# Gated linear attention: the TensorE pieces of two heads interleaved, the scores issued in front of the state updates

## The chip, the cores and the metric

The kernel runs on one core of one Trainium2 chip. The metric is device time in microseconds (us), the median over runs. The engines are named as the profile names them: PE is the matrix engine (TensorE), PEld its weight loads, DVE the vector engine, ACT the scalar engine, POOL the engine GpSimd, and SP the engine that issues the DMAs. PE writes its products to PSUM, which has eight banks of 128 x 512 float32; this kernel gives four of them to a pool "pm" and four to a pool "pd".

## The reference

One encoder layer is computed for two sequences of 512 tokens (a "prompt" and a "sample", called s = 0 and s = 1 in the kernel), model width 1024: a half-step SwiGLU, then a mixer of two head groups, then a second half-step SwiGLU and a gated per-layer embedding, each with a layer norm. The change lies in one of the mixer's head groups, the bidirectional gated linear attention with 4 heads, key width 64, value width 128, in chunks of 64 tokens (8 chunks a sequence). Cut to what matters, one direction of one head is:

```python
scores = einsum('bnihd,bnjhd->bnhij', q * exp(cum - mid), k * exp(mid - cum))
scores = where(mask, scores, 0.0)                       # triangle of each chunk
o_intra = einsum('bnhij,bnjhe->bnihe', scores, v)
upd = einsum('bnjhd,bnjhe->bnhde', k * exp(last - cum), v)
state_{n+1} = chunk_decay_n[..., None] * state_n + upd_n   # over the 8 chunks, in order
o_inter = einsum('bnihd,bnhde->bnihe', q * exp(cum), state_n)
o = o_intra + o_inter
```

The forward and the backward direction are added, normalised per head (RMS), multiplied by a gate, and go with the attention heads' output into one output projection `w_out`.

## The kernel before, in words

**PE's order is written out by hand.** The order of all other engines is set by the scheduler of the tile framework, which also hands out buffers from pools and adds the waits. Python generators each issue one piece of PE work (with the work of other engines that belongs to it) and then yield. A `Ticker` steps the main stream: one tick is three matmuls of a projection. `weave` takes one piece of a side stream, then as many ticks as keep the two in step up to a target tick.

In the stage of the change the main stream is the output projection (`wout`, the matmuls at line L703): the attention heads' half for both sequences, then, from tick 384 on, the linear attention's half for s = 0. The side stream is `order()`: 64 pieces woven into the 81 ticks from 334 to 415, so that after a piece there are one or two ticks, 1.27 on average.

**One sequence of the linear attention** is four generators in `gla(s)`:

- `pre(hp)`, five pieces for a pair of heads: loads, then four times two small matmuls (L986), whose exponentials (ACT, L173) scale queries and keys. The scaled `qk1` of both heads (q1, k1, both directions stacked on the partitions) is written by DVE at L1004.
- `one(h)`, three pieces for a head. First: the loads of the values `gvh` and the gates `Gh` (L1012, L1013, eight DMAs on SP), the transposes of k1 (L1018) and the copy of the result to `kT` (ACT, L1020). Second: the eight state updates U = kT x gvh (L1025, two banks), then the chain of states `W`: two copies on ACT (L1032, L1033), six forward and six backward steps on DVE that depend on one another (L1035, L1037), and two multiplications by the decay on POOL (L1038, L1039). Third: the scores S (L1047, two banks) and their masked copy into `A` (DVE, L1049).
- `two_a(h)`, one piece: the output o, one bank, twelve matmuls (L1058 with A and gvh, L1061 with q1 and the states W); then a square on ACT (L1064), a sum on DVE (L1066), the RMS (DVE L778, ACT L173, DVE L183 to L185), and four DVE instructions that write the gated result to `Gh` (L1069).
- `two_b(h)`, one piece: the transposes of `Gh` (L1076), and their copies into `mixG` (ACT L1077, DVE L1078), which the output projection reads.

The texts below call the pieces of a pair of heads 0 and 1: kT0, U0, S0, kT1, U1, S1 (the three pieces of `one`), o0 and o1 (`two_a`), p (the five of `pre` for the next pair; the first holds loads alone), t0 and t1 (`two_b`). A pair is 15 pieces, the last pair (which has no `pre` behind it) 10, with three empty pieces ahead of its last transposes. Before the change a pair's order was

```python
yield from A[1](0)      # kT0 U0 S0
yield from A[1](1)      # kT1 U1 S1
yield from A[2](0)      # o0
yield from A[2](1)      # o1
yield from A[0](1)      # p p p p p
yield from A[3](0)      # t0
yield from A[3](1)      # t1
```

There are four pairs: two for s = 0 (`A`) and two for s = 1 (`B`). The products of the pieces kT, U, S, o, p and t all take banks of the pool pd, four in number; a piece that asks for a bank waits until the last reader of some earlier product is done.

Of the kernel before, what the change touches and what calls it, by code (L numbers as in the profile page):

```python
# [20 lines left out]
NT = 4  # L21
# [9 lines left out]
PLAN = dict(s0=102,  # L31
            s1=112,
            d0=(8, 14, 20, 26, 32),
            sB=(52, 56, 60, 75, 77),
            d1=(90, 96, 102, 108, 117),
            A=(157, 159, 160),
            seg=((2, 132), (2, 142), (18, 160), (18, 170), (43, 193), (43, 216), (178, 334)),
            b=(4, 3),
            end=415)
# [671 lines left out]
class Middle:  # L711
# [246 lines left out]
    def gla(self, s):  # L958
        nc, L = self.nc, self.L
        f, bw = slice(0, 64), slice(64, 128)  # L960
        T = {}
# [45 lines left out]
        def one(h):  # L1007
            cs = slice(h * 128, (h + 1) * 128)
            gv = self.m2("gvh", shape=(128, NT, 128))
            G = self.m2("Gh", shape=(128, NT, 128))  # L1010
            for t in range(NT):
                nc.sync.dma_start(gv[:, t], self.spill["gv", s][t][:, cs])  # L1012
                nc.sync.dma_start(G[:, t], self.spill["G", s][t][:, cs])  # L1013
            q1, k1 = T["z", h][:, 0], T["z", h][:, 1]
            R = T["R", h]
            b = L.bank_d()
            for t in range(NT):
                nc.tensor.transpose(b[:, t * 128:(t + 1) * 128], k1[:, t * 128:(t + 1) * 128], L.ident)  # L1018
            kT = self.m2("kT", shape=(128, NT, 128))
            nc.scalar.activation(kT.rearrange("p a n -> p (a n)"), b, AF.Copy)  # L1020
            yield
            U = [L.bank_d().rearrange("p (c n) -> p c n", c=4) for _ in range(2)]
            for c in range(8):
                rw = slice(64 * (c % 2), 64 * (c % 2) + 64)
                nc.tensor.matmul(U[c % 2][:, c // 2], kT[rw, c // 2], gv[rw, c // 2], start=True, stop=True)  # L1025
            if h % 2 == 0:
                T["W"] = self.m8("W", (128, 2, 8, 128))
            W = T["W"][:, h % 2]
            nc.gpsimd.memset(W[f, 0], 0.0)
            nc.gpsimd.memset(W[bw, 7], 0.0)  # L1030
            up = lambda c, rd: U[c % 2][rd, c // 2]
            nc.scalar.activation(W[f, 1], up(0, f), AF.Copy)  # L1032
            nc.scalar.activation(W[bw, 6], up(7, bw), AF.Copy)  # L1033
            for c in range(1, 7):
                nc.vector.scalar_tensor_tensor(W[f, c + 1], W[f, c], R[f, c:c + 1], up(c, f), ALU.mult, ALU.add)  # L1035
                cb = 7 - c
                nc.vector.scalar_tensor_tensor(W[bw, cb - 1], W[bw, cb], R[bw, cb:cb + 1], up(cb, bw), ALU.mult, ALU.add)  # L1037
            nc.gpsimd.tensor_tensor(W[f, 1:8], W[f, 1:8], R[f, 1:8].unsqueeze(2).to_broadcast([64, 7, 128]), ALU.mult)  # L1038
            nc.gpsimd.tensor_tensor(W[bw, 0:7], W[bw, 0:7], R[bw, 0:7].unsqueeze(2).to_broadcast([64, 7, 128]), ALU.mult)  # L1039
            yield  # L1040
            A = T["A"][:, h % 2]
            S = [L.bank_d().rearrange("p (a n) -> p a n", a=NT) for _ in range(2)]
            for t in range(NT):
                ts = slice(t * 128, (t + 1) * 128)
                for dr in range(2):
                    rd = slice(64 * dr, 64 * dr + 64)
                    nc.tensor.matmul(S[dr][:, t], k1[rd, ts], q1[rd, ts], start=True, stop=True)  # L1047
            for dr in range(2):
                nc.vector.copy_predicated(A, self.L.mask[:, dr].unsqueeze(1).to_broadcast([128, NT, 128]), S[dr])  # L1049
            T["h", h] = gv, G, W, A  # L1050
            yield

# [84 lines left out]
def build(tc, d, outs):  # L1137
    nc = tc.nc
    ctx = ExitStack()
    with ctx:  # L1140
# [37 lines left out]
        with ExitStack() as mctx:  # L1178
            M = Middle(L, mctx, h1)
            o0, q0, o1, q1 = [], [], [], []  # L1180

            def projections():
                yield from M.akvz(0, o0)
                yield from M.aq(0, q0)
                yield from M.g_gr(0)
                yield from M.g_gr(1)
                yield from M.akvz(1, o1)
                yield from M.aq(1, q1)
                yield from M.g_gv(0)
                yield from M.g_gqk(0)  # L1190
                yield from M.g_gv(1)
                yield from M.g_gqk(1)
                yield from M.wout(0, 1)
                yield from M.wout(1, 1)
                yield from M.wout(0, 0)
            main = Ticker(projections())
            main.to(28)
            main.weave(L.flip(1, 1, "h1T"), 8, 60)

            def rows1():  # L1200
                m = M.m8("h1", (128, 4, 512))
                for c in (slice(0, 512), slice(512, 1024)):
                    for j in range(2):
                        src = d["lnw"][j:j + 1, c]
                        nc.sync.dma_start(m[:, j], src.partition_broadcast(128).rearrange("p a n -> p (a n)"))
                    for n in range(2 * NT):
                        s, t = divmod(n, NT)
                        h = m[:, 2 + n % 2]
                        nc.sync.dma_start(h, z1[s][t][:, c])
                        L.affine(h, m[:, 0], m[:, 1])  # L1210
                        nc.sync.dma_start(h1[s][t][:, c], h)
                        if n % 2:
                            yield
            main.weave(rows1(), 8, 100)
            main.to(PLAN["s0"])
            main.weave(M.qk_stacks(0, q0, o0[0], (None, 0, 1, 2, 3)), 5, PLAN["s1"])
            main.to(130)
            M.preload()
            A, B = M.gla(0), M.gla(1)
            A00 = A[0](0)  # L1220
            attn = M.attn((o0[1], o1[1]), lambda: main.n > 256)
            sB = M.qk_stacks(1, q1, o1[0], (0, 1, 2, None, 3))
            d0, d1 = M.decay(0, o0[2]), M.decay(1, o1[2])
            ins = sorted([(k, d0) for k in PLAN["d0"]] + [(k, sB) for k in PLAN["sB"]] + [(k, d1) for k in PLAN["d1"]]
                         + [(k, A00) for k in PLAN["A"]], key=lambda x: x[0])
            side = merge(attn, ins)
            p = 0
            for k, n in PLAN["seg"]:
                main.weave(side, k - p, n)
                main.to(n)  # L1230
                p = k
            assert next(side, None) is None, p
            def order():
                yield from A00
                for _ in range(PLAN["b"][0]):
                    yield
                yield from A[1](0)
                yield from A[1](1)
                yield from A[2](0)
                yield from A[2](1)  # L1240
                yield from A[0](1)
                yield from A[3](0)
                yield from A[3](1)
                yield from A[1](2)
                yield from A[1](3)
                yield from A[2](2)
                yield from A[2](3)
                yield from B[0](0)
                yield from A[3](2)
                yield from A[3](3)  # L1250
                yield from B[1](0)
                yield from B[1](1)
                yield from B[2](0)
                yield from B[2](1)
                yield from B[0](1)
                yield from B[3](0)
                yield from B[3](1)
                yield from B[1](2)
                yield from B[1](3)
                yield from B[2](2)  # L1260
                yield from B[2](3)
                for _ in range(PLAN["b"][1]):
                    yield
                yield from B[3](2)
                yield from B[3](3)
            main.weave(order(), 60 - len(PLAN["A"]) + PLAN["b"][0] + PLAN["b"][1], PLAN["end"])
            main.end()

            def ln2(s, fast):
                m, r = L.ln_scale(s, LN_EPS, fast)  # L1270
                for t in range(NT):
                    L.ln_z(s, t, m, r)
                    nc.sync.dma_start(z2[s][t], L.Y[s, t])
            ln2(0, True)
            main = Ticker(M.wout(1, 0))
            main.to(14)
            raw = L.rest()
            main.weave(L.flip(0, 2, "h2T", raw), 8, 32)
            main.end()
            ln2(1, False)  # L1280
# [164 lines left out]
```

## Time and profile before

| | us |
|---|---|
| median of 3 runs | 2014.57 (2014.25 to 2017.84) |
| the profiled execution's own time | 2012.7 |
| its span, first to last instruction | 2010.6 |
| PE busy in the span | 1893.7 (94%) |
| DVE busy | 1379.6 (69%) |
| the four pairs of heads, from 1038.19 to 1170.68 | 132.49 |
| PE busy in them | 115.17 |
| DVE busy in them | 108.39 |

The profile is of one execution. Starts and durations in a timeline row are in us from the span's start; a bracket at the end of a row is the idle time of that engine just before the row and what ended it. A group "x4" is four like instructions in a row, and a matmul's end is modelled, so that neighbouring groups overlap a little. In a row of stretches come the stretch, its length, the busy time of PE, PEld, DVE, ACT and POOL with their instruction counts, the TensorE clock granted (1.00 is full speed), and the DMA share and GB/s.

### The profile page before, as it was taken

Reading aid. Unit: us, or ns where it says so; the run is one execution under the profiler, and the core shown is the slowest. Engines: PE = TensorE matmul, PEld = TensorE weight load, DVE = VectorE, ACT = ScalarE, POOL = GpSimd, SP = SyncE. Lnnn points to the kernel's source line nnn. Section 1 sums busy time; section 2 is a strip of 40 time slices with the busy share of each in tenths; the row PEclk is TensorE's granted clock in tenths of the full one; section 3 lists DMA queues with packets and bytes.
Section 4 is the critical chain, followed back from the end, with each engine's and each line's share of the span. In section 5 each row is a group of like instructions: output and inputs, shape, how many; then the busy total and the mean of one; then the engine's idle time right before and its main releaser. Section 6 shows DMA issues by size and latency. Waiting matters only on the chain. (4 is left out here: it accounts for less than half of the span.)

```text
span 2010.6 us, 25530 instructions
## 1 busy us (share of the span) xinstructions
PE 1893.7 (94%) x8838; PEld 1544.4 (77%) x8838; DVE 1379.6 (69%) x2100; ACT 883.1 (44%) x1670; POOL 945.1 (47%) x710
## 2 busy tenths in 40 slices
PE   7999999999899987989998898998999999799899
PEld 5788888888688766877876676877888888588687
DVE  7857566574565875788778888777566574645973
ACT  5445444444221534757744256335444444221342
POOL 0665665555671352342233345554665545841243
PEclk9999999999899998999999998999999999899999
DMA  4425434479664544222442233555434479466232
GB/s 175 152 105 182 167 139 168 163 271 355 250 235 164 178 157 160 84 79 89 142 142 89 90 132 120 179 172 198 164 137 168 158 292 351 184 239 240 74 116 84
DMA packets 119936, 339.02 MB, mean 169 GB/s; under 512 B 12672, under 2 KB 49280, under 8 KB 114432
## 3 DMA queue, kind: packets, MB, share of 16 engines
q1 hardware_dynamic: 119808, 337.39, 46.8%
q8 instruction: 70, 1.15, 0.2%
q14 instruction: 58, 0.48, 0.1%
HBM read 227.24 MB, written 110.10 MB: 168 GB/s over the span
## 5 line engine op out<-in xcount | busy, mean ns | idle before, releaser
L138 POOL TENSOR_TENSOR w<-raw,w 128x512 fp32r<-128x512 f32 (+1 forms) x372 | 507.9, 1376 | 802.6 <-ACT w L137 741.9
L137 ACT ACTIVATE w<-raw 128x512 fp32r<-128x512 f32 (+1 forms) x586 | 362.0, 624 | 426.5 <-PE pm L535 91.3
L424 PE MATMUL pm<-X,w 128*128 128x512 f32 x1848 | 439.0, 395 | 21.3 <-ACT X L137 8.1
L424 PEld LDWEIGHTS pm<-X,w 128*128 128x128 f32 x1848 | 350.1, 190 | 101.8 <-ACT X L137 8.8
L266 POOL TENSOR_TENSOR raw<-raw 128x512 f32<-128x512 f32 x240 | 346.3, 1452 | 165.1 <-DMA raw<-in_wgu 96.4
L424 PE MATMUL pd<-X,w 128*128 128x512 f32 x1320 | 310.7, 394 | 2.9 <-DVE w L138 2.2
L138 DVE TENSOR_TENSOR w<-raw,w 128x512 fp32r<-128x512 f32 x214 | 218.8, 1028 | 113.4 <-ACT w L137 103.6
L424 PEld LDWEIGHTS pd<-X,w 128*128 128x128 f32 x1320 | 249.6, 189 | 58.5 <-DVE w L138 3.0
L535 PE MATMUL pm<-w,XB 128*128 128x512 f32 x864 | 205.6, 399 | 14.2 <-issue 7.5
L535 PEld LDWEIGHTS pm<-w,XB 128*128 128x128 f32 x864 | 166.3, 193 | 51.8 <-issue 7.8
L703 PE MATMUL pm<-w,h1T 128*128 128x512 f32 (+1 forms) x768 | 183.9, 383 | 16.2 <-ACT gr L745 16.2
L138 DVE TENSOR_TENSOR hs<-sg,hs 128x512 fp32r<-128x512 f32 (+1 forms) x182 | 145.2, 818 | 46.6 <-ACT hs L137 45.3
L137 ACT ACTIVATE hs<-sg 128x512 fp32r<-128x512 f32 (+1 forms) x182 | 98.5, 562 | 172.4 <-DVE sg L387 67.9
L703 PEld LDWEIGHTS pm<-w,h1T 128*128 128x128 f32 x768 | 137.0, 196 | 38.2 <-ACT gr L745 16.4
L535 PE MATMUL pd<-w,XB 128*128 128x512 f32 x648 | 151.6, 393 | 6.4 <-DVE Y L522 5.7
L535 PEld LDWEIGHTS pd<-w,XB 128*128 128x128 f32 x648 | 122.6, 190 | 33.4 <-DVE Y L522 6.9
L522 DVE TENSOR_TENSOR Y<-Y,pm 128x512 f32<-128x512 f32 x104 | 70.7, 684 | 63.7 <-PE pm L535 63.6
L522 DVE TENSOR_TENSOR Y<-Y,pd 128x512 f32<-128x512 f32 x88 | 59.7, 683 | 53.6 <-PE pd L535 50.0
L703 PE MATMUL pm<-w,h3T 128*128 128x512 f32 x384 | 91.3, 397 | 0.0
L703 PEld LDWEIGHTS pm<-w,h3T 128*128 128x128 f32 x384 | 73.1, 192 | 15.2
L367 DVE TENSOR_TENSOR sg<-u,pm 128x512 f32<-128x512 f32 x22 | 15.1, 687 | 99.0 <-PE pm L424 99.0
L648 ACT ACTIVATE pd<-pd,c_lnT 128x512 f32<-128x512 f32 x48 | 36.1, 756 | 91.3 <-PE pd L646 89.6
(239 smaller groups left out, 2575.7 us busy)
## 6 DMA issues: line engine op xcount, KB each, us to landing
hs<-hs SPq DMA_DIRECT2D x126, 512.0 KB, 2.6
XB<-hs SPq DMA_DIRECT2D x42, 1536.0 KB, 7.3
raw<-in_wgu SPq DMA_DIRECT2D x88, 512.0 KB, 3.4
raw<-in_wd SPq DMA_DIRECT2D x36, 512.0 KB, 6.8
hs_t<-hs SPq DMA_DIRECT2D x56, 256.0 KB, 2.5
XB<-hs_t SPq DMA_DIRECT2D x26, 512.0 KB, 5.2
raw<-in_wout SPq DMA_DIRECT2D x16, 512.0 KB, 3.5
raw<-in_wpg SPq DMA_DIRECT2D x16, 512.0 KB, 3.6
```

The source lines that it names most:

```text
L137: nc.scalar.activation(hi, raw, AF.Copy)
L138: (eng or nc.vector).tensor_tensor(lo, raw, hi.bitcast(F32), ALU.subtract)
L266: (sums or self.nc.gpsimd).tensor_tensor(o(), x(), y(), ALU.subtract)
L367: add = lambda o, x, y: nc.vector.tensor_tensor(o, x, y, ALU.add)
L424: nc.tensor.matmul(bank, w[:, a, kt * 128:(kt + 1) * 128], X[k][:, kt, b], start=(k in (0, 1, 4) and kt == 0 and m == 0), stop=(kt == 3 an ...
L522: nc.vector.tensor_tensor(yv, yv, bank, ALU.add)
L535: nc.tensor.matmul(b[t], h[:, a, t * 128:(t + 1) * 128], d[:, c], start=(k in (0, 4, 1) and g == 0 and x == 0), stop=(g == len(H) - 1 and ...
L648: nc.scalar.activation(p, p, AF.Identity, scale=self.lnT[:, c:c + 1], bias=self.lnT[:, c + 8:c + 9])
L703: nc.tensor.matmul(banks[t][:, :width], x[:, i, t * 128:(t + 1) * 128], w[a][:, j], start=(q == 0 and a == 0 and m == 0), stop=(q == nq - ...
```

## The change

Two things are done, both to PE's written order. Inside `one(h)` the scores S with their masked copy come as the second piece and the state updates U as the third. And the order of a pair's pieces is no longer head after head: a function `two` takes the generators of both heads and steps them in turn. In the names above the order of a pair goes

- from: kT0 U0 S0 kT1 U1 S1 o0 o1 p p p p p t0 t1
- to: kT0 S0 U0 kT1 S1 o0 U1 t0 o1 p p p p p t1

No instruction is added or removed. The number of pieces and the ticks between them stay as they were; in the last pair the three empty pieces stand ahead of t1 alone, where they stood ahead of t0 and t1. The whole diff:

```diff
@@ gla(s), one(h)
             kT = self.m2("kT", shape=(128, NT, 128))
             nc.scalar.activation(kT.rearrange("p a n -> p (a n)"), b, AF.Copy)
             yield
+            A = T["A"][:, h % 2]
+            S = [L.bank_d().rearrange("p (a n) -> p a n", a=NT) for _ in range(2)]
+            for t in range(NT):
+                ts = slice(t * 128, (t + 1) * 128)
+                for dr in range(2):
+                    rd = slice(64 * dr, 64 * dr + 64)
+                    nc.tensor.matmul(S[dr][:, t], k1[rd, ts], q1[rd, ts], start=True, stop=True)
+            for dr in range(2):
+                nc.vector.copy_predicated(A, self.L.mask[:, dr].unsqueeze(1).to_broadcast([128, NT, 128]), S[dr])
+            yield
             U = [L.bank_d().rearrange("p (c n) -> p c n", c=4) for _ in range(2)]
             for c in range(8):
...
             nc.gpsimd.tensor_tensor(W[f, 1:8], W[f, 1:8], R[f, 1:8].unsqueeze(2).to_broadcast([64, 7, 128]), ALU.mult)
             nc.gpsimd.tensor_tensor(W[bw, 0:7], W[bw, 0:7], R[bw, 0:7].unsqueeze(2).to_broadcast([64, 7, 128]), ALU.mult)
-            yield
-            (the ten lines of A, S, the matmuls and the copies, as above)
             T["h", h] = gv, G, W, A
             yield
@@ build, order()
-                yield from A[1](0)
-                yield from A[1](1)
...
-                yield from B[3](2)
-                yield from B[3](3)
+                def two(H, p, nxt):
+                    g = [H[1](p), H[1](p + 1)]
+                    for j in (0, 0, 0, 1, 1):
+                        next(g[j])
+                        yield
+                    yield from H[2](p)
+                    next(g[1])
+                    yield
+                    yield from H[3](p)
+                    yield from H[2](p + 1)
+                    yield from nxt
+                    for _ in range(PLAN["b"][1] if nxt is last else 0):
+                        yield
+                    yield from H[3](p + 1)
+                last = ()
+                yield from two(A, 0, A[0](1))
+                yield from two(A, 2, B[0](0))
+                yield from two(B, 0, B[0](1))
+                yield from two(B, 2, last)
```

More of the change, by code (lines that the diff above doesn't have):

```diff
@@ L1039, in one @@
             nc.gpsimd.tensor_tensor(W[bw, 0:7], W[bw, 0:7], R[bw, 0:7].unsqueeze(2).to_broadcast([64, 7, 128]), ALU.mult)
-            yield
[L1041 to L1049, printed above, removed]
             T["h", h] = gv, G, W, A
@@ L1236, in order @@
                     yield
-                yield from A[1](0)
-                yield from A[1](1)
[L1239 to L1262, printed above, removed]
-                    yield
-                yield from B[3](2)
-                yield from B[3](3)
+                def two(H, p, nxt):
[5 more added lines that the diff above has]
+                    next(g[1])
+                    yield
+                    yield from H[3](p)
[9 more added lines that the diff above has]
+                yield from two(B, 2, last)
             main.weave(order(), 60 - len(PLAN["A"]) + PLAN["b"][0] + PLAN["b"][1], PLAN["end"])
```

## The prediction

> **What bounds the kernel now.** I read the page first, for the engine that is nearly always busy, then the stretches of the four pairs of heads, then who PE waited for in them.
>
> ```profile
> span 2010.6 us, 25530 instructions
> PE 1893.7 (94%) x8838; PEld 1544.4 (77%) x8838; DVE 1379.6 (69%) x2100; ACT 883.1 (44%) x1670; POOL 945.1 (47%) x710
> ```
>
> PE is the bound: whatever makes PE wait, or run at a lower clock, goes into the time one for one. The stage of the change, by pairs of heads (from one kT0 to the next, the last to the end of its t1):
>
> ```profile
> 1038.19:1071.44 33.25, 28.98 (x201) 21.36 (x202) 26.94 (x66) 12.70 (x32) 13.94 (x14) 1.00 0.36 113
> 1071.44:1104.62 33.18, 28.98 (x202) 21.37 (x202) 28.24 (x67) 11.02 (x30) 15.21 (x13) 1.00 0.31 92
> 1104.62:1138.65 34.03, 29.46 (x202) 21.65 (x202) 27.82 (x69) 11.40 (x31) 13.05 (x12) 1.00 0.41 122
> 1138.65:1170.68 32.03, 27.74 (x174) 19.73 (x175) 25.39 (x62) 7.52 (x17) 12.64 (x12) 0.89 0.22 78
> ```
>
> PE is busy 28.98 of 33.25 us in a pair and idle for 4 to 5; DVE with 26.94 is not far behind. So a better order can win at most some 4.3 us a pair, 17 in all. The waits of PE between 1030 and 1175 us (who, total, times, longest):
>
> ```profile
> PE pd L1018 <- DVE W L1035: 7.5, 4, 3.1
> PE pd L1018 <- DVE qk L1004: 5.5, 4, 1.8
> PE pd L1058 <- DVE W L1035: 4.4, 4, 1.3
> ```
>
> The first is kT1, which reads no W: it waits for a bank of pd, the one of head 0's state updates, until the chain has read it. The third is o0, likewise for a bank of U1, since its own states were ready long before (below). The second is kT0 of each pair, waiting for the scaled keys out of `pre`. Now the first pair on PE, row by row:
>
> ```profile
> 1038.19 0.63 PE L1018 MATMUL pd<-c_ident,qk 128*128 128x128 f32 x4 [1.02 <-DVE qk L1004]
> 1038.58 0.95 PE L703 MATMUL pm<-w,mixA 128*128 128x512 f32 x3
> 1039.51 1.16 PE L1025 MATMUL pd<-gvh,kT 64*128 64x128 f32 x16
> 1040.60 1.66 PE L703 MATMUL pm<-w,mixA 128*128 128x512 f32 x6
> 1042.19 1.16 PE L1047 MATMUL pd<-qk 64*128 64x128 f32 x16
> 1043.28 0.96 PE L703 MATMUL pm<-w,mixA 128*128 128x512 f32 x3
> 1045.57 0.63 PE L1018 MATMUL pd<-c_ident,qk 128*128 128x128 f32 x4 [1.33 <-DVE W L1035]
> 1045.95 0.94 PE L703 MATMUL pm<-w,mixA 128*128 128x512 f32 x3
> 1046.89 1.16 PE L1025 MATMUL pd<-gvh,kT 64*128 64x128 f32 x16
> 1047.98 0.97 PE L703 MATMUL pm<-w,mixA 128*128 128x512 f32 x3
> 1048.88 1.16 PE L1047 MATMUL pd<-qk 64*128 64x128 f32 x16
> 1049.97 1.66 PE L703 MATMUL pm<-w,mixA 128*128 128x512 f32 x6
> 1052.95 0.46 PE L1058 MATMUL pd<-gvh,A 128*128 128x128 f32 x2 [1.32 <-DVE W L1035]
> ...
> 1056.07 0.97 PE L703 MATMUL pm<-w,mixA 128*128 128x512 f32 x3
> 1056.87 0.38 PE L1058 MATMUL pd<-gvh,A 128*128 128x128 f32 x2
> ...
> 1065.55 0.61 PE L986 MATMUL pd<-c_U,lq 128*128 128x132 f32 x4
> ...
> 1071.44 0.63 PE L1018 MATMUL pd<-c_ident,qk 128*128 128x128 f32 x4 [1.62 <-DVE qk L1004]
> ```
>
> From starts to starts: kT 0.39 (1038.19 to 1038.58), U and S 1.09 each, two ticks 1.59, so 0.8 a tick, and o 3.12 (1052.95 to 1056.07). One tick stands behind each piece, two behind the second, sixth, tenth and thirteenth.
>
> **What the change moves, part by part.** The price on which all hangs is how long after U the states W can be read. Their last two steps are on POOL:
>
> ```profile
> 1042.41 2.50 POOL L138 TENSOR_TENSOR w<-raw,w 128x512 fp32r<-128x512 f32 x2 [2.07 <-issue]
> 1045.51 1.68 POOL L1038 TENSOR_TENSOR W<-W,R 64x896 f32<-64x896 f32 x1 [0.59 <-DVE W L1035]
> 1047.26 1.68 POOL L1039 TENSOR_TENSOR W<-W,R 64x896 f32<-64x896 f32 x1
> ```
>
> U0 starts at 1039.51, W0 is ready at 1047.26 + 1.68 = 1048.94: **9.4 us from the start of U**, all in series (ACT, the DVE chain, POOL twice). Before, 13.4 us of PE's order lie between U0 and o0 (1039.51 to 1052.95), so the chain is covered; and o1, 10.0 us after U1 (1046.89 to 1056.87), still fits. The change puts only kT1 and S1 between U0 and o0, and only t0 between U1 and o1.
>
> The second price is what o leaves behind it: the gated result, which t reads.
>
> ```profile
> 1059.33 1.13 DVE L1069 SCALAR_TENSOR_TENSOR Gh<-pd,gny,Gh 128x128 f32<-128x128 f32 x4
> ...
> 1064.72 1.13 DVE L1069 SCALAR_TENSOR_TENSOR Gh<-pd,gny,Gh 128x128 f32<-128x128 f32 x4
> ```
>
> o0 ends at 1056.07, its result is there at 1059.33 + 1.13 = 1060.46: 4.4 us. The second result ends at 1065.85, and the next kT0 starts at 1071.44: 5.6 us later, and 5.9 after the last piece of `pre` (1065.55).
>
> The first pair in the new order, kT0 at 0:
>
> - S0 comes first, so the copy of kT is hidden: S0 1.2 to 2.3, two ticks, U0 3.9 to 5.0, a tick, kT1 5.8 to 6.2 (its bank is now one that the masked copy frees early: the 7.5 us of the first wait row go), a tick, S1 7.0 to 8.1, a tick: o0 could start at 8.9.
> - W0 is ready at 3.9 + 9.4 = 13.3. **PE waits 4.4 us**, of which 0.4 can hold o0's first product (A with gvh needs no W). o0 ends at 13.3 + 3.1 - 0.4 = 16.0.
> - Two ticks, U1 17.6 to 18.7, a tick to 19.5. t0 needs o0's result, 16.0 + 4.4 = 20.4: 0.9 of waiting; t0 and a tick to 21.6.
> - o1 needs W1: 17.6 + 9.4 = 27.0, and about 1 us more because the last DVE work of o0's result (1.13) falls where the chain wants to start: 28.1. **PE waits 6.5 us.** What is queued behind it is the whole main stream. o1 ends at 28.1 + 2.7 = 30.8.
> - Then seven ticks (5.6) and the four pieces of `pre` (0.4 each) to 37.9, t1 and ticks to 39.9. The next kT0 needs the scaled keys: 5.6 after o1's result (30.8 + 4.4 = 35.2) gives 40.8; 5.9 after the last piece of `pre` (37.5) gives 43.4. In the old order both rows name the same 5.6 to 5.9 us; here the first DVE input is early and PE's is late, so the truth lies between. I take 41.5, nearer the first, because that stretch is mostly DVE work in a queue.
>
> So a pair takes 41.5 us for a mean of 33.5 in the first three rows: +8.0, three times, 24.0. The last pair has no `pre` behind it: o1 ends at 30.8, its result is ready at 35.2, t1 ends at 35.6, against 32.03: +3.6. Together **+27.6**. Bounds: 40.8 and 43.4 for the next kT0 give 25.5 and 33.3.
>
> **The clock.** A PE that waits that long does not come back at full speed. The one long wait of the old order (3.1 in the first row of waits; PE was busy for 0.70 us from 1144.00 on, then idle until 1147.8) shows the price:
>
> ```profile
> 1144.00:1147.00 3.00, 0.70 (x3) 0.22 (x2) 2.74 (x9) 0.00 (x0) 0.10 (x1) 1.00 0.49 172
> 1147.00:1149.00 2.00, 1.18 (x5) 1.21 (x6) 1.91 (x5) 0.06 (x1) 1.25 (x1) 0.60 0.01 4
> 1149.00:1151.00 2.00, 2.00 (x11) 1.25 (x12) 1.61 (x3) 0.54 (x1) 1.93 (x2) 0.50 0.00 0
> 1151.00:1153.00 2.00, 2.00 (x14) 1.68 (x13) 0.17 (x1) 0.54 (x2) 0.18 (x1) 0.50 0.00 0
> 1153.00:1155.00 2.00, 2.00 (x18) 1.25 (x17) 1.84 (x6) 0.00 (x0) 0.00 (x0) 0.70 0.00 0
> ```
>
> Half clock from the end of that wait on: 2 us at 0.60 are 1.6 at half, then 2 and 2, and 1.2 at 0.70, in all 6.8 us, which costs up to 3.4. Both new waits are longer. After the first, o0, two ticks and U1 (5.4 us of work, all on the way to W1) run in that half-speed stretch: I take 2.7. Of the second, 6.1 us long, part of the half-speed stretch passes while PE still waits, and o1 runs in the rest: 1.6. Bounds are 0 and 3.4 for each, so 0 to 6.8 a pair; 4.3 in four pairs is **+17.2**. In the last pair the old order paid such a stretch already; it stands in its 32.03.
>
> [...]
>
> **Edits with one answer.** No DMA is added, and none passes another: the loads of a head stay in its first piece, which for both heads stands where it stood (first and fourth). The tiles of a pair held at o0 are six (values and gates of both heads, kT1, the square), the six buffers that there are. The two masked copies come ahead of the chain on DVE, not behind it, while PE is at the two ticks and U0 itself (2.7 us): nothing. If that cover were gone, the chain would start later by two DVE instructions over a bank each, less than what rival 4 adds. Three empty pieces ahead of t1 alone: nothing, t1 is late by its result.
>
> **The sum.** 2010.6 + 27.6 + 17.2 = 2055.4 of span; the profiled execution's own time is 2.1 above its span (2012.7), and the median 1.9 above that (2014.57): 2059.4. I say **2059**.
>
> **The rivals.**
> 1. Faster: the interleaving hides the chain. Then the first and third waits go, 11.9 us, and the time is 2002.7. It decides at o0: W0 would have to be there within the 5.0 us that U0, kT1, S1 and three ticks give (3.9 to 8.9). POOL's two instructions alone take 3.4 of that. 4 in 100. No change (the waits only change places, 2014): PE's order is written by hand, so it will change; 3 in 100.
> 2. The waits come, but the clock holds: 2014.57 + 27.6 = 2042. For it: waits of 1.8 and less in the rows of waits left the clock at 1.00 in the first three pairs. Against: the new ones are two to three times that. 15 in 100.
> 3. [...] 15 in 100.
> 4. POOL's queue: a weight split of two (2.50, the first row of POOL) lands ahead of the decay multiplications. Before, PE did not need W soon; now 2.5 us once a pair go straight into PE's wait: 2059 + 10 = 2069. 9 in 100.
>
> My forecast itself: 52 in 100; the last 2 are for slower than all of these.
>
> **How the numbers follow.** 2059 is the likeliest case. The range runs from 2038, a little under the case without a clock loss (bounds 25.5 of waits), to 2074: the upper bound of the keys (33.3) with most of the clock's (6.8 a pair would be 27.2, together 2075). It takes in rivals 2, 3 and 4. Within 0.2% (4 us) a measurement of this kernel tells nothing from no change; faster by more 0.04, same 0.03, slower 0.93.
>
> **What would show it.** In the changed kernel's waits: L1018 on W gone; L1058 or L1061 waiting for POOL's W L1039, eight times, about 4 us at o0 and 6 at o1; L1076 waiting for Gh a little; kT0 still waiting for qk; pairs of 41 to 46 us in place of 33; a clock well under 1.00 in each. I am wrong if o0 or o1 do not wait for POOL (the chain is shorter than 9.4, or the framework orders DVE so that W is done first), or if the pairs stay under 36 us.

## The result and the profile after

| | before | after |
|---|---|---|
| median | 2014.41 us | 2072.46 us (2068.83 to 2073.72) |
| ratio, with its 95% interval | 1 | 1.0272 (1.0252 to 1.0292) |
| the profiled execution's own time | 2012.7 | 2068.83 |
| the four pairs of heads | 132.49 | 192.40 |

The change made the kernel 58 us slower; 45 were predicted (2059, range 2038 to 2074). The first lines of the page:

```profile
span 2066.6 us, 25528 instructions
PE 1916.4 (93%) x8838; PEld 1557.5 (75%) x8838; DVE 1377.7 (67%) x2100; ACT 882.2 (43%) x1670; POOL 944.8 (46%) x710
```

The work of DVE, ACT and POOL is the same as before to 0.2%. PE is busy 22.7 us longer with the same 8838 instructions: it ran part of them slower. The pairs of heads, in the columns used before (stretch, length, PE, PEld, DVE, ACT, POOL, clock granted, DMA share, GB/s):

```profile
1032.59:1079.14 46.55, 34.95 (x202) 25.15 (x202) 27.46 (x66) 12.21 (x30) 14.55 (x14) 0.82 0.28 80
1079.14:1128.24 49.10, 35.73 (x201) 25.31 (x202) 29.76 (x67) 11.31 (x30) 13.77 (x13) 0.79 0.26 75
1128.24:1180.40 52.16, 38.16 (x202) 27.55 (x202) 29.57 (x72) 11.49 (x32) 12.56 (x12) 0.76 0.25 71
1180.40:1224.99 44.59, 33.49 (x174) 23.46 (x175) 23.68 (x60) 7.40 (x17) 12.53 (x12) 0.74 0.20 65
sum 192.40, PE 142.33 PEld 101.47 DVE 110.47 ACT 42.41 POOL 53.41; mean PE 35.58 PEld 25.37 DVE 27.62 ACT 10.60 POOL 13.35
```

All of the loss is here: 59.9 us more than before. (The pairs begin 5.6 us earlier in this execution than in the one before, from parts that the change does not touch, so the span grew by 56.0.) Two things add up: PE is busy 142.33 instead of 115.17, 27.2 more, and idle 50.1 instead of 17.3, 32.8 more. The clock column gives the time at half clock, twice what is missing from 1.00 (cut into slices of 0.2 us, the time from 1030.2 to 1242.0 has 623 at 1.00, 416 at 0.50 and 20 between): 0.18 x 2 x 46.55 = 17 us, then 21, 25 and 23, in all some 86, where before there were 7, all in the last pair.

Who PE waits for from 1030 to 1240 us (who, total, times, longest), and the first pair on PE:

```profile
PE pd L1061 <- POOL W L1049: 37.0, 8, 6.4
PE pd L1018 <- DVE qk L1004: 9.5, 4, 4.4
PE pd L1058 <- DVE W L1045: 2.7, 4, 0.8
PE pd L1076 <- DVE Gh L1069: 1.9, 2, 1.2
```

```profile
1036.53 1.16 PE L1035 MATMUL pd<-gvh,kT 64*128 64x128 f32 x16
...
1042.51 0.49 PE L1058 MATMUL pd<-gvh,A 128*128 128x128 f32 x2 [0.75 <-DVE W L1045]
1046.08 0.52 PE L1061 MATMUL pd<-W,qk 128*64 128x128 f32 x4 [3.09 <-POOL W L1049]
...
1053.33 1.16 PE L1035 MATMUL pd<-gvh,kT 64*128 64x128 f32 x16
...
1062.88 0.70 PE L1061 MATMUL pd<-W,qk 128*64 128x128 f32 x4 [6.13 <-POOL W L1049]
...
1128.24 1.08 PE L1018 MATMUL pd<-c_ident,qk 128*128 128x128 f32 x4 [2.47 <-DVE qk L1004]
...
1180.40 1.09 PE L1018 MATMUL pd<-c_ident,qk 128*128 128x128 f32 x4 [4.36 <-DVE qk L1004]
```

(The lines of `one` have moved: U is L1035, POOL's multiplications are L1048 and L1049.) Both waits for W are where the prediction put them: 3.09 us at o0, behind 0.75 for a bank, and 6.13 at o1. In both heads of this pair o can read W 9.55 us after U started (1036.53 to 1046.08, 1053.33 to 1062.88). In the other pairs head 0 has 9.5 to 9.6 as well; head 1 has 11.4, 10.2 and 9.5. The rows of kT0 show what was not foreseen: its wait for the keys grows from pair to pair (1.02, 1.63, 2.47, 4.36), and the transposes behind the last two waits take 1.08 instead of 0.63. The clock around the two waits of the first pair:

```profile
1046.00:1050.00 4.00, 3.92 (x20) 2.34 (x20) 0.00 (x0) 0.00 (x0) 0.03 (x1) 0.54 0.01 3
1050.00:1054.00 4.00, 4.00 (x22) 2.76 (x23) 1.83 (x6) 1.01 (x3) 0.00 (x0) 0.61 0.06 16
1054.00:1058.00 4.00, 2.74 (x22) 2.12 (x18) 3.74 (x13) 1.86 (x4) 0.63 (x1) 1.00 0.17 49
1058.00:1062.00 4.00, 0.00 (x0) 0.00 (x0) 2.92 (x7) 0.00 (x0) 3.17 (x3) 0.75 0.00 0
1062.00:1066.00 4.00, 3.12 (x16) 1.89 (x16) 0.00 (x0) 0.00 (x0) 0.82 (x1) 0.50 0.00 0
1066.00:1070.00 4.00, 4.00 (x16) 2.77 (x13) 1.44 (x3) 1.23 (x2) 0.00 (x0) 0.50 0.00 0
1070.00:1074.00 4.00, 4.00 (x25) 3.51 (x24) 2.98 (x11) 1.84 (x7) 1.29 (x1) 0.97 0.40 105
```

Behind the first wait the clock is at half for 3.7 + 3.1 = 6.8 us, at the second for 2 (the row at 0.75) + 4 + 4 + 0.2 = 10.2. That one begins at about 1060, while PE still waits, and outlasts the wait's end (1062.88) by some 7 us.

### The profile page after: what moved, and what is told of

It is laid out like the page before. It is cut to its first block, busy times and chain, and to the rows that moved or that the text cites. A ratio compares the mean times of both kernels' runs of the same rounds, so it can differ in the third digit from the quotient of the medians.

```text
span 2066.6 us, 25528 instructions
## 1 busy us (share of the span) xinstructions
PE 1916.4 (93%) x8838; PEld 1557.5 (75%) x8838; DVE 1377.7 (67%) x2100; ACT 882.2 (43%) x1670; POOL 944.8 (46%) x710
## 5 line engine op out<-in xcount | busy, mean ns | idle before, releaser
L138 POOL TENSOR_TENSOR w<-raw,w 128x512 fp32r<-128x512 f32 (+1 forms) x372 | 506.6, 1372 | 838.5 <-ACT w L137 732.5
L138 DVE TENSOR_TENSOR w<-raw,w 128x512 fp32r<-128x512 f32 x214 | 213.7, 1004 | 116.0 <-ACT w L137 106.1
L703 PE MATMUL pm<-w,h1T 128*128 128x512 f32 (+1 forms) x768 | 182.8, 381 | 17.3 <-ACT gr L745 16.3
L138 DVE TENSOR_TENSOR hs<-sg,hs 128x512 fp32r<-128x512 f32 (+1 forms) x182 | 145.6, 820 | 46.5 <-ACT hs L137 45.2
```

The source lines that it names most:

```text
L138: (eng or nc.vector).tensor_tensor(lo, raw, hi.bitcast(F32), ALU.subtract)
L703: nc.tensor.matmul(banks[t][:, :width], x[:, i, t * 128:(t + 1) * 128], w[a][:, j], start=(q == 0 and a == 0 and m == 0), stop=(q == nq - ...
```

## The experiments

My theory: o0 stands too close behind U0, and o1 too close behind U1 (which now comes after o0), so PE waits for W, twice a pair, and each wait costs a second time through the clock. The rivals: the swap of S and U is itself what costs (its masked copies, its banks); or it is all wait and no clock; or the early t0 is the cause. The ratios are to the kernel before, run on the same chip; the changed kernel has 1.0272.

| kernel | median us | ratio (95%) |
|---|---|---|
| e1_scores_first | 2021.87 | 1.0031 (1.0016 to 1.0046) |
| e2_interleave_only | 2037.65 | 1.0117 (1.0090 to 1.0145) |
| e3_filled | 2058.57 | 1.0216 (1.0192 to 1.0240) |
| e3b_filled_more | 2051.21 | 1.0179 (1.0158 to 1.0200) |
| e4_decay_act | 2063.53 | 1.0242 (1.0219 to 1.0265) |
| e6_t0_back | 2070.82 | 1.0269 (1.0251 to 1.0287) |
| e7_u1_first | 2042.28 | 1.0124 (1.0104 to 1.0144) |
| e8_keys_pool | 2027.24 | 1.0040 (1.0005 to 1.0075) |
| e9_sum_on_act | 2013.27 | 0.9988 (0.9970 to 1.0006) |
| e10_first_split | 2016.07 | 1.0009 (0.9994 to 1.0024) |
| e11_after_split | 2066.28 | 1.0259 (1.0236 to 1.0283) |
| e12_split_sum | 2015.83 | 1.0007 (0.9996 to 1.0019) |

### e1_scores_first: the swap alone

The new `one` (S ahead of U) with the order head after head of before:

```diff
-  kT0 S0 U0 kT1 S1 o0 U1 t0 o1 p p p p p t1
+  kT0 S0 U0 kT1 S1 U1 o0 o1 p p p p p t0 t1
```

> One half of the change alone: inside a head the scores stand in front of the state updates, but the heads follow one another as before (kT0 S0 U0 kT1 S1 U1 o0 o1 p t0 t1). Theory A (the cost is PE waiting for the states W, 9.4 us after U starts, and the half clock behind such waits): U0 3.9, U1 8.9, o0 could start at 11.6 and waits 1.7 for W0 (13.3); o1 could start at 16.8 and waits about 2 for W1 (18.3 to 19.3); o1 ends near 22, where it ended at 21.7 before. So 2014 to 2022, and no half clock in most pairs. Theory B (the swap itself is at fault, since it starts each chain 2.4 us later): the chain of both heads goes on the path, about half of the 58 us, 2035 to 2050.

Measured: 2021.87, so the swap of S and U costs 6 us, not 58. PE's waits in the four pairs:

```profile
PE pd L1061 <- POOL W L1049: 10.1, 7, 3.0
PE pd L1035 <- DVE W L1045: 4.2, 4, 2.3
```

The 7.5 us that kT1 waited for a bank are gone, as they are in the changed kernel; in their place o waits for W, since U stands one piece nearer to it, and U1 waits for a bank of U0. The rival that the swap itself is the cause falls.

### e2_interleave_only: the order alone

U ahead of S as before, in the new interleaved order:

```diff
-  kT0 S0 U0 kT1 S1 o0 U1 t0 o1 p p p p p t1
+  kT0 U0 S0 kT1 U1 o0 S1 t0 o1 p p p p p t1
```

> The other half alone: the pieces of two heads interleaved in the new order, but with the state updates in front of the scores as before (kT0 U0 S0 kT1 U1 o0 S1 t0 o1 p t1). Theory A: U0 at 1.3 and U1 at 8.7 are so early that W0 (10.7) is there when o0 comes (10.6), and W1 (about 19) when o1 comes behind S1 and t0 (19.8): little waiting, 2014 to 2024. Theory B (the swap is at fault): 2014 as well. Theory C (the early t0 and the o0 work between the heads cost by themselves): 2040 and more.

Measured: 2037.65, 14 us beyond my theory's range and close to the third one's "2040 and more". What was said of o holds: no wait for POOL's W is left. But t0, to which my theory gave no price, waits for o0's result (who, total, times, longest):

```profile
PE pd L1076 <- DVE Gh L1069: 15.6, 5, 4.9
```

DVE's own rows of the first pair say why. o0's last product starts at 1052.32 and takes 0.44; its square, done at 1053.5, waits for its sum (L1066) behind the last step of head 1's chain, and then the masked copies of S1 come in between:

```profile
1053.71 0.35 DVE L1037 SCALAR_TENSOR_TENSOR W<-W,R,pd 64x128 f32<-64x128 f32 x1
1054.09 0.69 DVE L1066 TENSOR_REDUCE oss<-osq 128x4 f32<-128x512 f32 x1
...
1055.49 0.73 DVE L1049 COPY_PREDICATED A<-c_mask,pd 128x512 f32<-128x512 uint32 x1
...
1057.20 0.71 DVE L1049 COPY_PREDICATED A<-c_mask,pd 128x512 f32<-128x512 uint32 x1
...
1058.65 1.12 DVE L1069 SCALAR_TENSOR_TENSOR Gh<-pd,gny,Gh 128x128 f32<-128x128 f32 x4
```

The result is ready at 1059.77, 7 us after o0, where the prediction's rows have 4.4. An early t0 is a second place where PE catches up with a chain of another engine.

### e3_filled and e3b_filled_more: the waits kept, the clock held

The new kernel with matmuls that nobody needs (identity times gv, into o's own bank, overwritten by o) ahead of each o. They take no engine's result away and make no chain shorter; they only keep PE at work while it would wait.

```diff
+  for n in range(8 if h % 2 == 0 else 14):      # e3b: 13 and 26
+      nc.tensor.matmul(o[:, n % NT], L.ident, gv[:, n % NT], start=True, stop=True)
```

> The changed kernel with idle work put into PE's two long waits: ahead of each o, matmuls of the identity with gvh into the bank of o (8 for the even head, about 3.1 us; 14 for the odd one, about 5.5 us), overwritten by the products that follow. The result is the same; PE has 35 us more work. Theory A: the waits stay, but the clock stays at 1.00 in them; of the 85 us at half clock in the stage of the changed kernel most go, and the time falls by 20 to 32 us, to 2040 to 2052. If the half clock costs nothing (its work lies under other waits), the time stays at 2072 or rises.

Measured: 2058.57, 14 us better than the change but not the 20 to 32 expected. The filler was mis-sized: a matmul of it is two instructions of 0.12 us, so it lasted only 1.9 and 3.1 us (3.1 and 5.5 were meant), and o still waits 18.0 us in the four pairs, up to 3.2 at once. So once more, with 13 and 26:

> The changed kernel with more idle work in the two waits than in the run before (13 matmuls of the identity ahead of the even head's o, 26 ahead of the odd one's; 8 and 14 left waits of 1.3 and 3.2 us, 37.5 us at half clock and 2058.6). Theory A: half clock is left only behind the waits for the keys; the pairs take 41.5 to 43 us as the sum without a clock loss said, 2042 to 2052. If the idle work lies on the path by itself, 2058 or more.

Measured: 2051.21, within what the clock's theory expected. The pairs, their sum, and what is left of o's waits for W:

```profile
1039.27:1080.95 41.68, 38.18 (x280) 30.21 (x280) 27.19 (x66) 12.11 (x30) 14.87 (x14) 1.00 0.28 88
1080.95:1126.05 45.10, 39.70 (x280) 31.52 (x280) 30.26 (x67) 11.31 (x30) 13.77 (x13) 0.96 0.28 82
1126.05:1171.59 45.54, 39.86 (x279) 31.51 (x280) 29.84 (x72) 11.46 (x32) 12.56 (x12) 0.96 0.28 81
1171.59:1210.73 39.14, 36.49 (x252) 28.48 (x252) 23.58 (x60) 7.51 (x17) 12.61 (x12) 0.92 0.20 68
sum 171.46, PE 154.24 PEld 121.72 DVE 110.87 ACT 42.38 POOL 53.81; mean PE 38.56 PEld 30.43 DVE 27.72 ACT 10.60 POOL 13.45
```

```profile
PE pd L1063 <- POOL W L1049: 2.7, 7, 0.6
```

This splits the loss. The chains from U to W are on the whole no shorter than in the changed kernel (9.5 to 9.6 us in head 0; 10.4, 11.8, 10.1 and 10.0 in head 1, where the changed kernel has 9.6, 11.4, 10.2 and 9.5), PE even does more, and the pairs are 192.40 - 171.46 = 20.9 us shorter: that is the clock (21.3 by the medians, 18.7 by the two ratios). The other 39.0 (171.46 - 132.49) are waits and what is left of half clock, now only behind the waits of kT0. By the clock column that is 0.04 x 2 x 45.10 = 3.6 us in the second pair, then 3.6 and 6.3, in all 13.5 us at half clock; the kernel before had 7, and a us at half clock costs at most half a us, so this adds at most 3 us to the loss. (The last row ends 0.2 us short of the end of t1.)

### e7_u1_first: U1 ahead of o0

```diff
-  kT0 S0 U0 kT1 S1 o0 U1 t0 o1 p p p p p t1
+  kT0 S0 U0 kT1 S1 U1 o0 t0 o1 p p p p p t1
```

> The changed kernel with one other piece put back: U1 ahead of o0 (kT0 S0 U0 kT1 S1 U1 o0 t0 o1 p t1), so that W1 is made while o0 runs. Theory A: the wait at o1 (some 6 us in each pair) and most of the half clock go; o0 waits 2 to 3 for W0. What is left beside the run with the scores first alone (2022) is the early t0, which then has the chain of head 1 and its masked copies ahead of its input on DVE and waits 3 to 5 us in a pair, as it did with the interleaving alone (2038): 2028 to 2045. If U1's place is not the cost, 2060 to 2072.

Measured: 2042.28, 30 us of the 58 back from exchanging two neighbours, o0 and U1. o no longer waits for W (0.7 us in all); t0's wait for o0's result takes its place:

```profile
PE pd L1076 <- DVE Gh L1069: 17.8, 5, 4.5
PE pd L1061 <- POOL W L1049: 0.7, 3, 0.2
```

With e1, which differs from e7 by t0's place alone, the loss falls apart into steps, by ratios: the swap of S and U 6 us (0.31%), t0 ahead of o1 another 19 (0.93%), U1 behind o0 another 30 (1.48%).

### e6_t0_back: t0 behind `pre` again, U1 still behind o0

```diff
-  kT0 S0 U0 kT1 S1 o0 U1 t0 o1 p p p p p t1
+  kT0 S0 U0 kT1 S1 o0 U1 o1 p p p p p t0 t1
```

> The changed kernel with one piece put back: t0 behind the pieces of pre again (kT0 S0 U0 kT1 S1 o0 U1 o1 p t0 t1). Theory A (the place of U1 behind o0 is the cost): t0 filled a part of a wait that ends with W1 anyway, so moving it back makes that wait longer by as much: 2066 to 2074, no change. Theory C (the early t0, which waits for the result of o0, is the cost): 2050 or less.

Measured: 2070.82, no change that can be told from the changed kernel. The waits only moved: kT0's for the keys fall from 9.5 to 3.5, o's for W rise by the same 6:

```profile
PE pd L1061 <- POOL W L1049: 43.2, 8, 9.2
PE pd L1018 <- DVE qk L1004: 3.5, 3, 1.7
```

So t0's 19 us are not on top of U1's: while o1 waits for W1 anyway, t0 only fills part of that wait. Taken in this order, from e1 to e6 and on to the changed kernel, U1's place costs 48 us (1.0031 to 1.0269) and t0's nothing. Each of the two alone is enough to make a pair late, and what a step costs depends on which was taken first.

### e4_decay_act and e11_after_split: a shorter chain

Two tries at shortening the 9.5 us from U to W in the changed kernel: the two multiplications as fourteen small ones on ACT, each right behind its step of the chain; and POOL's two cut in four, of which the first two can start half-way through the chain.

```diff
 e4:
+  nc.scalar.activation(W[f, c], W[f, c], AF.Identity, scale=R[f, c:c + 1])
+  nc.scalar.activation(W[bw, cb], W[bw, cb], AF.Identity, scale=R[bw, cb:cb + 1])
+  (in the loop of the chain; behind it the same two for W[f, 7] and W[bw, 0])
-  nc.gpsimd.tensor_tensor(W[f, 1:8], ...)
-  nc.gpsimd.tensor_tensor(W[bw, 0:7], ...)
 e11:
+  if c == 4: (the same two on W[f, 1:5] and W[bw, 3:7])
-  nc.gpsimd.tensor_tensor(W[f, 1:8], ...)
-  nc.gpsimd.tensor_tensor(W[bw, 0:7], ...)
+  (the same two on W[f, 5:8] and W[bw, 0:3])
```

> The changed kernel with a shorter chain: the decay multiplications of W, two POOL instructions of 1.68 us behind the DVE chain, are done on ACT chunk by chunk, each as soon as the chain is past that chunk (14 small ACT instructions, two of them behind the chain's end). W is ready about 7.0 us after U starts and not 9.4. Theory A: each of the eight waits gets 2.4 us shorter, 19 us, and with waits of 1.4 and 3.7 fewer half-clock stretches, 5 to 20 us more: 2033 to 2049. If something else than the chain's end holds o (DVE's order, banks), the time stays at 2072.

Measured: 2063.53, 9 us better than the change (6 by the ratios, whose intervals overlap a little) instead of 23 to 39. The group of the forward multiplications (48 of them in the four pairs, busy time and mean ns), and PE's wait:

```profile
L1048 ACT ACTIVATE W<-W,R 64x128 f32<-64x128 f32 x48 | 19.2, 400 | 2.6 <-DVE W L1045 2.1
```

```profile
PE pd L1063 <- ACT W L1051: 28.7, 7, 5.6
```

A small multiplication on ACT is 0.40 us, where ACT's copies of that shape take 0.27. Fourteen are 5.6 us a head, one after the other, so they fall behind the chain's steps that they should keep up with, and ACT is its end in POOL's place: in the first head W is ready 8.6 us after U started (1045.05 to 1053.64), not the 7.0 expected.

> The changed kernel with the two decay multiplications on POOL cut in four: chunks that the DVE chain has left (f 1 to 4, bw 3 to 6) are multiplied while it goes on, the other three of each behind its end. Less work stands behind the chain: two instructions of some 0.75 us in place of two of 1.68, so W is ready about 1.9 us earlier, eight times. Theory A: 15 us of waiting less, and some of the half clock with it: 2048 to 2058. ACT in that place won 9 us, because its 14 small instructions took longer than the chain. If the end of the chain is not what o waits for, 2072.

Measured: 2066.28, 6 us better than the change by the medians and 3 by the ratios, which is within their intervals, instead of 14 to 24. PE's waits for W fall from 37.0 to 31.5 us in all, not by 15. POOL's rows in the first pair, head 0 and head 1:

```profile
1044.28 1.04 POOL L1049 TENSOR_TENSOR W<-W,R 64x512 f32<-64x512 f32 x1 [1.81 <-DVE W L1045]
...
1047.40 0.82 POOL L1052 TENSOR_TENSOR W<-W,R 64x384 f32<-64x384 f32 x1
1059.64 1.26 POOL L138 TENSOR_TENSOR w<-raw,w 128x512 fp32r<-128x512 f32 x1 [11.41 <-issue]
```

In four parts the work takes 3.9 us from start to end (1044.28 to 1048.22), in two it took 3.4 before (1045.51 to 1048.94), so of the half that runs early little is gained; and in head 1 a weight split (L138) stands ahead and takes the time of the early half. That is the fourth rival's mechanism; here it costs at most its own 1.26 us.

### e8_keys_pool, e9_sum_on_act, e10_first_split, e12_split_sum: is there a version that beats both?

What was left to win are the waits of the order head after head. Four tries: the keys' product of every second head on POOL (e8, before's code), the sum of squares by ACT's accumulation (e9, before's code), e1 with the split of e11 (e10), and e10 with e9 (e12).

```diff
 e8:
-  nc.vector.tensor_tensor(z[rd, e, i], ...)
+  (nc.gpsimd if e else nc.vector).tensor_tensor(z[rd, e, i], ...)
 e9, e12:
-  nc.scalar.activation(sq, o, AF.Square)
-  nc.vector.tensor_reduce(ss, sq, AX.X, ALU.add)
+  for t in range(NT):
+      nc.scalar.activation(sq[:, t], o[:, t], AF.Square, accum_out=ss[:, t:t + 1])
```

> Not the change: the kernel before, with the four multiplications a pair that scale queries and keys of the odd head moved from DVE to POOL, which is idle for more than half of a pair. If DVE's queue sets when the next kT0 can start (its waits are 5.5 us in the kernel before) and how far the chains lie behind, 2005 to 2012. If POOL and DVE slow one another when both read and write SBUF (the three multiplications beside a POOL weight split took 4.12 us where three alone took 2.0), nothing is won: 2013 to 2022.

> Not the change: the kernel before, with the sum of squares of o taken by ACT's own accumulation (four squares of 128 columns) in place of a DVE reduction of 0.69 us: 1.4 us of DVE less in a pair. If DVE's queue sets the pace of a pair (27 of 33 us busy), 2009 to 2013; if only the order of dependent pieces does, 2014 to 2017.

> The scores in front inside each head, heads one after the other (2022 as it stood, with 10.1 us of waits at o for POOL's last multiplication), and POOL's decay multiplications cut in four as above. Those waits get up to 1.9 us shorter, seven times: 2011 to 2016, level with or a little under the kernel before. If the waits move on to DVE's queue instead, 2017 to 2022.

> The two edits that came out level with the kernel before, together: scores in front inside each head with POOL's decay multiplications cut in four (2016.1, ratio 1.0009), and the sum of squares taken by ACT (2013.3, ratio 0.9988). If the waits at o (6.8 us) and at U1 (4.4 us) that the first still has come through DVE's queue, 1.4 us less of DVE in a pair shortens them: 2008 to 2013, faster than before by a little. If they come from the order of dependent pieces alone, 2013 to 2017, no change.

e8 is slower, by 0.05 to 0.75%; its six runs spread from 2010.67 to 2035.08, and their median lies above both ranges. Its groups for L1004 from 1030 to 1175 us, and below them the one of the kernel before:

```profile
L1004 POOL TENSOR_TENSOR qk<-lq,E 64x512 f32<-64x512 f32 x16 | 25.6, 1614 | 9.0 <-issue 6.7 <-ACT E L173 1.8 <-POOL w L138 0.2
L1004 DVE TENSOR_TENSOR qk<-lq,E 64x512 f32<-64x512 f32 x16 | 16.8, 1057 | 0.9 <-ACT E L173 0.7
```

```profile
L1004 DVE TENSOR_TENSOR qk<-lq,E 64x512 f32<-64x512 f32 x32 | 25.1, 807 | 0.4
```

A product is 1.61 us on POOL, and DVE's own half takes 1.06 in place of 0.81, so kT0 waits 8.0 us for keys instead of 5.5. e9, e10 and e12 are level with before: each interval holds 1. e9 and e10 fall between their two ranges and decide nothing about DVE's queue. In e10 the split takes e1's wait of o for W from 10.1 to 6.8 us, and of e1's loss of 0.31% some 0.09% is left. e12 agrees with its second case, that the order of dependent pieces sets what is left. No version here is shown to beat before.

## Why the prediction was right, and where its sizes were off

- **The chain from U to W.** Predicted 9.4 us in series; measured 9.5 to 9.6 in head 0 of every pair and in head 1 of the first. The first pair was followed to the end of the first wait almost exactly: o0 reads W at 13.3 us after kT0 by the prediction, at 13.5 by the trace (1032.59 to 1046.08). The first wait was put at 4.4 and is 0.75 for a bank, 0.49 of A with gvh, and 3.09: 4.3.
- **The microsecond that DVE was to add at W1** did not come in the first pair of the changed kernel: at half clock U1 itself came later (20.7 us after kT0 instead of 17.6), and head 1's chain could start when o0's result was just written. There U1 to o1 is 9.55 like U0 to o0, and the second wait, 6.1 predicted, is 6.13 all the same. In the second pair the microsecond came, and more: o0's result is written until 1103.90, only then does head 1's chain start, and U1 to o1 takes 11.4 (1100.18 to 1111.56). In e3b, at full clock, the first pair has 10.4, where the prediction has 10.5.
- **A pair without the clock, 41.5 us**, taken between 40.8 and 43.4. e3b is the run to compare with. Its PE rows of the first pair, and the lengths of the parts of all four pairs:

```profile
1043.21 1.16 PE L1035 MATMUL pd<-gvh,kT 64*128 64x128 f32 x16
...
1052.76 0.44 PE L1063 MATMUL pd<-W,qk 128*64 128x128 f32 x4 [0.18 <-POOL W L1049]
...
1057.09 1.16 PE L1035 MATMUL pd<-gvh,kT 64*128 64x128 f32 x16
...
1067.49 0.44 PE L1063 MATMUL pd<-W,qk 128*64 128x128 f32 x4 [0.49 <-POOL W L1049]
```

| part, us | predicted | pair 1 | pair 2 | pair 3 | pair 4 |
|---|---|---|---|---|---|
| kT0 to U0 | 3.9 | 3.9 | 5.5 | 5.5 | 6.8 |
| U0 to o0's first product with W | 9.4 | 9.6 | 9.6 | 9.5 | 9.6 |
| from there to U1 | 4.3 | 4.3 | 4.3 | 4.3 | 4.3 |
| U1 to o1's first product with W | 10.5 | 10.4 | 11.8 | 10.1 | 10.0 |
| from there to the next kT0 (pair 4: to the end of t1) | 13.4 (7.5) | 13.5 | 13.9 | 16.2 | 8.4 |
| whole pair | 41.5 (35.6) | 41.7 | 45.1 | 45.5 | 39.1 |

The first pair is the predicted one, part by part. The step that failed is the one that multiplies it: "a pair takes 41.5 us (...): +8.0, three times". The four pairs together are 11.3 us longer than predicted, which turns the 27.6 into 39 (36 without the half clock that e3b has beyond the kernel before). Of the 11.3 us, 6.0 lie between kT0 and U0, where the clock is at half behind the wait for the keys; 4.3 lie behind o1, most of them in the third pair. The price for that last part, 5.6 us from o1's result to the next kT0, was read in the first pair of the kernel before alone. The other two pairs of that kernel have 6.5 and 6.9 (1098.11 to 1104.62, 1131.76 to 1138.65), and e3b has 5.3, 7.3 and 7.0. That t0 no longer stands ahead of kT0 is not the cause: with t0 back there (e6) kT0's wait falls, but o1's rises by as much, and the time stays.

- **The clock, 17.2 us**: e3b measures 21 (18.7 by the ratios). That a wait of some 3 us is enough held: 3.09 us in the changed kernel (0.75 for a bank just ahead of it), as 3.1 us in the kernel before. Too small were the length of a stretch (up to 10.2 us, where I had taken the 6.8 that before showed), and their number: I counted two a pair, and the waits at kT0 bring two more.
- **The sum.** 36 to 39 of waits and 21 to 24 of clock make the 59.9 of the pairs; 44.8 were predicted. Both terms were too small, by three to four tenths and by a fifth to two fifths. The waits lie outside their own bounds, 25.5 to 33.3; the range held, with 1.5 us to spare, because its upper end adds most of the clock's bound to theirs. The mechanism is the predicted one; that the total stayed inside is in part luck.
- **The rivals.** The first falls: o waits for W all eight times. The second (the clock holds, 2042) falls by the rows around 1046, and with it any case in which the clock holds through the shorter wait: 0.54 stands right behind the 3.09 us. The fourth, POOL's queue, gave 2069, the number nearest to the measured one, but its mechanism is not there: weight splits of 1.3 and 2.5 us do land ahead of L1048 in the changed kernel, yet in all eight heads POOL is done with them at least 0.5 us before DVE's chain ends, and waits for it.
- **The masked copies ahead of the chain**, priced at nothing, cost nothing. DVE's rows of the first pair of the changed kernel: the last copy of S0 is done 1.6 us before the chain can start (the bracket names a DMA; ACT's copies of U0, which the chain reads, are done at 1038.3 only).

```profile
1035.95 0.74 DVE L1030 COPY_PREDICATED A<-c_mask,pd 128x512 f32<-128x512 uint32 x1
1038.32 0.34 DVE L1045 SCALAR_TENSOR_TENSOR W<-W,R,pd 64x128 f32<-64x128 f32 x1 [1.64 <-DMA lq<-sp_l]
```

## What to carry to other kernels

Where one engine's order is written by hand, measure how long each hand-over takes from the piece that starts a chain on other engines to the piece that reads its end, and keep at least that much work between the two: here 9.5 us from U to W and 4.4 (7 when DVE is busy) from o to t. When a price is read from one repetition of a stage, look at the others before multiplying it: the 5.6 us of the first pair were 6.5 and 6.9 in the next two. When a piece is moved, look at both places: t0 put back took 6 us from kT0's waits and gave them to o's. Here the waits of PE, the bounding engine, cost a second time through its clock, 21 us beside 36 to 39, and useless matmuls that kept it at work were worth these 21 us, though the better cure was to move U1, worth 30.

## What the runs showed of the hardware

- **Short waits halved the clock.** In e3b a wait of 1.95 us, with PE at 0.05 us of work in two, was enough: the clock column falls to 0.84 and 0.50 right behind it. Before, the wait of 1.62 us ahead of the second pair left that pair at 1.00.

```profile
1079.00:1081.00 2.00, 0.05 (x1) 0.08 (x2) 1.91 (x4) 0.73 (x2) 2.00 (x2) 1.00 0.00 0
1081.00:1083.00 2.00, 2.00 (x15) 1.59 (x17) 1.97 (x3) 0.97 (x3) 0.94 (x1) 0.84 0.22 18
1083.00:1085.00 2.00, 2.00 (x14) 1.68 (x13) 1.76 (x3) 0.04 (x1) 0.79 (x4) 0.50 0.74 250
```

- **Stretches at half clock went on long after PE was at work again.** After the first wait in the changed kernel, of 3.09 us, the stretch lasted 6.8 us, with PE busy for all but 0.1 of the eight us in its rows; at the second, of 6.13 us, 10.2. The changed kernel has ten such stretches in its four pairs, one of 3.4 us, three of 6.8 and six of 10.2; the longer two lengths are close to two and three times the shortest. How much idle time starts a stretch, and how much work ends one, was not measured.
- **ACT's multiplication in place** of 64 x 128 took 0.40 us where its copy of that shape out of PSUM took 0.27 (L1043 in the trace of e4).
